# One stream step on one core: the sample moved from chunk 3 to chunk 2, fewer kept weights, the second norm's splits put ahead, v transposed one tile later

## The chip, the cores and the metric

One core of a Trainium2 chip runs the whole kernel. The metric is the device time of one execution in microseconds, the median of several.

## What is computed

One layer of a streaming encoder on 2048 prompt tokens (no history) and a sample of 8 sequences of 16 tokens, each with its own states and caches. The width is 1024, the feed-forward width 2816, all in float32:

```python
u = rms_norm(x, norm_mix) @ w_in                 # one projection, columns split among 4 mixers
z, xbc, dt_raw, q, k, v, u_sc, u_cc = jnp.split(u, IN_SPLITS, axis=-1)
ya, ssm_buf_new, h_new = mixer_ssd(z, xbc, dt_raw, ssm_buf, h0, ...)   # conv of 4 taps, then a scan in blocks
yb = swa_prompt(q, k, v, swa_sinks)              # or swa_sample(q, k, v, k_cache, v_cache, swa_sinks)
yc, sc_new = mixer_shortconv(u_sc, sc_buf, sconv_w)                    # conv of 3 taps
yd, cc_new = mixer_conformer(u_cc, cc_buf, ...)                        # conv of 31 taps
x = x + jnp.concatenate([ya, yb, yc, yd], axis=-1) @ w_out
hf = rms_norm(x, norm_ffn)
x = x + (jax.nn.silu(hf @ w_gate) * (hf @ w_up)) @ w_down
```

The results are the final norm of both token groups and the new states, among them the last 3 columns of `xbc` (`o_xc_s` for the sample) and the last 30 of the conformer's input (`o_g_s`).

## The kernel before

The 16 blocks of 128 prompt tokens are cut into five chunks, c0 to c4, and the sample's 128 tokens are appended to one of them. Tokens lie along the free axis, features along the partitions. Every matrix product is made from operands split into a high and a low part, in three matmuls for each 128 rows: high by high, high by low, low by high (`group`, L239 to L241). A split is a copy on ACT and a subtraction on DVE (`split`, L199; `split_w` for weights, L204, both with the subtraction through `tt`, L184). A weight tile of 128 x 1024 is loaded by SP into one of two buffers `fr` and split into one of three buffers `w`; or it was written in its split form to DRAM by POOL the first time (`kept<-w`, L227, 1 MB) and is later loaded from there (`w<-kept`, L219), without a split. `keep` says which tiles of w_in are stored so: in chunk 1 those with an even number, in chunk 2 those with an odd one.

The stages in order: proj_in of c0 and part of c1; for c0 and c1 in turn, proj_out, proj_in of the next chunk with the second norm beside it, and the chunk's FFN with the mixers of the next chunk woven in; proj_out of c2; the FFN of c2 merged with proj_in of c3, whose mixers run in it; the same for c4; then an FFN for the tokens of c3 and c4 together, with seven products in place of eight. proj_in runs over the 21 tiles of w_in, in c1 and c2 in the order of `W_IN_TILES` (c0, h0, b0, c1, h1, b1, k, v, B, C, dt, q0, q1, x0, x1, z0, z1, g0, a0, g1, a1; even and odd numbers in turn), in c3 and c4 in the order `SPREAD` (g0, a0, B, C, x0, x1, ...).

The tiles h, B, C, x0, x1 and a go through a buffer `raw` (two of them): DVE copies the last columns of the chunk before into its head (`raw_tiles`, L394), POOL loads the sample's history (L397, from `sst`, `xst` or `gst`), ACT or DVE puts in the new columns (`evac_raw`, L420 and L422), DVE keeps the last columns (`keep_raw`, L427), POOL stores the sample's last columns (L436, `o_xc_s<-raw`, 12 KB in pieces of 12 bytes), and the taps of the convolution are multiplied in one by one (`conv`, L187 and L192), for the prompt and the sample apart. A `raw` buffer is free for the next tile when its store has landed. For a0 and a1 DVE also doubles the loaded history (L191).

The second norm (`norm2`) makes the eight operands of the FFN: a multiply on DVE into `nt` and a split into `act`, two of them after each of four units of proj_in. v is transposed on TensorE right after its tile is computed (L569), from a copy that ACT makes into `ut` (L560).

A scheduler sets each engine's order when the kernel is built: it follows the order in the code, and `tc.high_priority(offset=n)` puts what is under it ahead as though it had been written n instructions earlier (AHEAD is 1000, used for weight loads with their splits, SOON is 120). Each engine and each DMA queue (SP's and POOL's) then runs in its order, and an instruction that waits holds all behind it.

The largest chunk has 512 tokens, `TM`; the FFN of the last two chunks works on halves of N = 448 tokens, whose operands come back from DRAM in tiles `ht`.

Of the kernel before, what the change touches and what calls it, by code (L numbers as in the profile page):

```python
# [17 lines left out]
P = 128  # L18
# [47 lines left out]


class Cfg:
    def __init__(self, chunks=(2, 4, 4, 3, 3), sample_in=3, nff=22, rounds=(4, 4, 4, 4, 3, 3),
                 rounds_last=(4, 4, 4, 4, 1, 3, 2), nfirst=3):  # L70
        self.chunks = chunks
        self.sample_in = sample_in
        self.nff = nff
        self.rounds = rounds
        self.rounds_last = rounds_last

        self.nfirst = nfirst
        self.np_tiles = sum(chunks)
        self.tokens = self.np_tiles * P + NS
        self.tmax = max(c * P + (NS if i == sample_in else 0) for i, c in enumerate(chunks))  # L80
# [38 lines left out]
def stream_step(ctx: ExitStack, tc: tile.TileContext, cfg, x, xr, w_in, w_out, w_gu, w_down, tab, con, dist_p, dist_s,  # L119
# [86 lines left out]
        return d  # L206

    kept = {}  # L210

    def load_w(src, shape, key=None, store=False):
# [15 lines left out]
        return pat(d[:, 0, :n]), pat(d[:, 1, :n])  # L228

    def keep(c, n):  # L230
        return c["i"] in (1, 2) and (c["i"] == 2 or n % 2 == 0)

    tail = [None]

# [212 lines left out]
    def after_in(c, name, ps):  # L447
# [18 lines left out]
        elif name[0] == "c":  # L466
            t = mk(up, [P, TM], "ut", bufs=B["ut"])[:, :T]
            act.activation(t, ps[:, :T], AF.Copy)
            u[name] = t
        elif name[0] == "h":  # L470
            j = int(name[1])
            rp, rs = raw_tiles(c, 2, hist["s"][j], sst[j])
            t = u["c" + name[1]]
            tt(rp[:, 2:2 + Tp], t[:, :Tp], ps[:, :Tp], ALU.mult)
            if Ts:
                tt(rs[:, :, 2:], sv(t[:, Tp:]), sv(ps[:, Tp:T]), ALU.mult)
            keep_raw(c, rp, rs, 2, hist["s"][j], o_s_p[j], o_s_s[j])
            m = mk(up, [P, TM], "mix", bufs=B["mix"])
            conv(c, m, rp, rs, [T_("sw", 3 * j + k) for k in range(3)], None)
            u["y" + name[1]] = m  # L480
        elif name[0] == "b":
            m = u["y" + name[1]]
            tt(m[:, :T], m[:, :T], ps[:, :T], ALU.mult)
        elif name in ("x0", "x1", "B", "C"):
            j = ("x0", "x1", "B", "C").index(name)
            rp, rs = raw_tiles(c, 3, hist["xs"][j], xst[j])
            evac_raw(c, ps, rp, rs, 3)
            keep_raw(c, rp, rs, 3, hist["xs"][j], o_xc_p[j], o_xc_s[j])
            m = mk(up, [P, TM], "x" + name)
            conv(c, m, rp, rs, [H_("xw", 4 * j + k) for k in range(4)], H_("xb", j))  # L490
            t = mk(up, [P, TM], "ut", bufs=B["ut"])[:, :T]
            act.activation(t, m[:, :T], AF.Tanh)
            stt(m[:, :T], t, 1.0, m[:, :T], ALU.add, ALU.mult)
            u[name] = m
        elif name == "dt":
            xx = mk(up, [P, TM], "ut", bufs=B["ut"])[:, :T]
            e = mk(up, [P, TM], "ut", bufs=B["ut"])[:, :T]
            l = mk(up, [P, TM], "acum")[:, :T]
            p = mk(up, [P, TM], "pk")[:, :T]

            act.activation(xx, ps[:, :T], AF.Identity, bias=T_("dtb"))
            act.activation(e, xx, AF.Abs)
            act.activation(e, e, AF.Exp, scale=-1.0)
            act.activation(l, e, AF.Ln, bias=1.0)
            ts(p, e, 0.2, ALU.mult)
            for cst in (-0.25, 1.0 / 3.0, -0.5, 1.0):
                stt(p, p, cst, e, ALU.add, ALU.mult)
            tt(p, p, l, ALU.subtract)
            stt(p, e, 0.05, p, ALU.is_lt, ALU.mult)
            tt(l, l, p, ALU.add)  # L510
            stt(xx, xx, 0.0, l, ALU.max, ALU.add)

            ts(e, xx, A, ALU.mult)
            for b in range(c["nt"]):
                bs_ = slice(b * P, (b + 1) * P)
                dve.tensor_tensor_scan(out=l[:, bs_], data0=ones, data1=e[:, bs_], initial=0.0, op0=ALU.mult,
                                       op1=ALU.add)
            if Ts:
                dve.tensor_tensor_scan(out=l[:, Tp:], data0=C_("rsts", P), data1=e[:, Tp:], initial=0.0,
                                       op0=ALU.mult, op1=ALU.add)  # L520
            u["acum"] = l

            for b in range(c["nt"]):
                act.activation(p[:, b * P:(b + 1) * P], l[:, b * P:(b + 1) * P], AF.Exp, scale=-1.0,
                               bias=l[:, b * P + P - 1:b * P + P])
            if Ts:
                lv, pv = sv(l[:, Tp:]), sv(p[:, Tp:])
                tt(pv, bc(lv[:, :, DEC_T - 1:], [P, DEC_B, DEC_T]), lv, ALU.subtract)
                act.activation(p[:, Tp:], p[:, Tp:], AF.Exp)
            tt(p, p, xx, ALU.mult)  # L530

            ts(p, p, C_("pick", 3)[:, 2:3], ALU.mult)
            stt(p, xx, C_("pick", 3)[:, 1:2], p, ALU.mult, ALU.add)
            stt(p, l, C_("pick", 3)[:, 0:1], p, ALU.mult, ALU.add)
            u["pk"] = p
        elif name in ("q0", "q1"):
            t = mk(up, [P, TM], name)
            act.activation(t[:, :Tp], ps[:, :Tp], AF.Copy, scale=0.125)
            if Ts:

                if name == "q0":
                    u["qs"] = mk(up, [P, DEC_B, 2, DEC_T], "qs")
                act.activation(u["qs"][:, :, int(name[1])], sv(ps[:, Tp:T]), AF.Copy, scale=0.125)
            u[name] = t
        elif name == "k":
            t = mk(up, [P, P + TM], "k")
            if prev["k"]:
                pool.tensor_copy(t[:, :P], hk)
            act.activation(t[:, P:P + T], ps[:, :T], AF.Copy)
            if c["i"] != last:  # L550
                pool.tensor_copy(hk, t[:, Tp:Tp + P])
            prev["k"] = True
            if Ts:
                pool.dma_start(o_k_s, t[:, P + Tp:P + T])
            if c["i"] == last:
                pool.dma_start(o_k_p, t[:, Tp:Tp + P])
            u["k"] = t
        elif name == "v":
            t = mk(up, [P, TM], "ut", bufs=B["ut"])[:, :T]
            act.activation(t, ps[:, :T], AF.Copy)  # L560
            if Ts:
                pool.dma_start(o_v_s, t[:, Tp:])
            if c["i"] == last:
                pool.dma_start(o_v_p, t[:, Tp - P:Tp])

            pv = mk(px, [P, 512], "px")
            nt = T // P
            for b in range(nt):
                pe.transpose(pv[:, b * P:(b + 1) * P], t[:, b * P:(b + 1) * P], ident)  # L569
            vt = mk(up, [P, 5, P], "vt", bufs=1)  # L570
            if prev["v"]:
                dve.tensor_copy(vt[:, 0], hv)
            act.activation(vt[:, 1:1 + nt].rearrange("p a b -> p (a b)"), pv[:, :T], AF.Copy)
            if c["i"] != last:
                dve.tensor_copy(hv, vt[:, c["nt"]])
            prev["v"] = True
            u["vt"] = vt
        elif name in ("z0", "z1"):
            t = mk(up, [P, TM], name)
            act.activation(t[:, :T], ps[:, :T], AF.Tanh, scale=0.5)  # L580
            stt(t[:, :T], t[:, :T], 1.0, ps[:, :T], ALU.add, ALU.mult)
            u[name] = t
# [290 lines left out]
    def proj_in(c, names):  # L873
        c.setdefault("u", {})

        def unit(name):
            wh, wl = load_w(w_in[W_IN_TILES.index(name)], [KT, P], W_IN_TILES.index(name), keep(c, W_IN_TILES.index(name)))
            ps = mk(pm, [P, 512], "pm")
            group(ps, c["T"], [(wh[:, k], wl[:, k], c["xn"][k]) for k in range(KT)])
            after_in(c, name, ps)  # L880

        return [lambda n=n: unit(n) for n in names]
# [27 lines left out]
    def norm2(c):  # L910
        T = c["T"]
        r = rstd_of(c["ss"], T, D)
        yield
        r = spread(r, T)
        c["hf"] = []
        for k in range(KT):
            t = mk(np_, [P, TM], "nt", bufs=B["nt"])[:, :T]
            stt(t, c["x2"][k][:, :T], T_("gffn", k), r, ALU.mult, ALU.mult)
            d = mk(ap, [P, 2, TM], "act", F32R)
            split(d, t, T)  # L920
            c["hf"].append(d)
            if k in (1, 3, 5):
                yield
        yield
# [333 lines left out]
    def operand(j, h):  # L1258
        if j >= cfg.nff - 2:
            d = hs[j, h]  # L1260
        else:
            with tc.high_priority(offset=AHEAD):
                d = mk(ht, [P, 2, N], "ht", F32R)
                sync.dma_start(d.bitcast(F32), hmem[j][:, h])
        return d[:, 0], d[:, 1]

# [192 lines left out]
```

## Time and profile before

| | |
|---|---|
| time, three runs | 2401.3, 2409.1 and 2415.3 us; median 2409.1 |
| the profiled execution | 2405.4 us, span 2403.7 |
| granted clock of TensorE, mean | 0.990 |
| proj_in of c2 | 508 to 626 us |
| FFN of c1 with the mixers of c2 | 626 to 1018 |
| proj_out of c2 | 1018 to 1057 |
| proj_in of c3 merged with the FFN of c2 | 1057 to 1431 |
| proj_out and proj_in of c4 | 1431 to 1680 |

Times in a view count from the span's start. PE is TensorE's matmuls, PEld its weight loads, DVE, ACT, POOL and SP the other engines and SP's queue. A row of a wait names the instruction that waited, after the arrow the engine and instruction that released it, then the total, the number of times and the longest.

### The profile page before, as it was taken

How to read it: one execution, taken by the hardware profiler on the slowest of the kernel's cores; microseconds unless marked ns; L12 is line 12 of the kernel's file. 1: busy time of each engine (PE TensorE's matmuls, PEld its weight loads, DVE VectorE, ACT ScalarE, POOL GpSimd, SP SyncE). 2: the span in 40 equal slices, each digit the busy share in tenths (PEclk: the TensorE clock that was granted, in tenths of full speed). 3: DMA queues.
4: the chain of work that ended last, by engine and by line, in shares of the span. 5: the costliest groups of instructions: out<-in, count | busy, mean ns of one | idle time of the engine just before them, and what ended most of it. 6: DMA issues, size and time to landing. Idle time of an engine off the chain costs nothing.

```text
span 2403.7 us, 32336 instructions
## 1 busy us (share of the span) xinstructions
PE 2348.2 (98%) x12370; PEld 2039.3 (85%) x12370; DVE 1580.0 (66%) x2980; ACT 883.2 (37%) x1500; POOL 148.0 (6%) x266
## 2 busy tenths in 40 slices
PE   8999999999999999997999999999999999999997
PEld 7888999888888888886778788988879999999997
DVE  7997998865884456657573554775777666763424
ACT  6544545533333333323212232232344444442221
POOL 1000000000000000001010000000001000000000
PEclk9999999999999999998999999999999999999998
DMA  6547454567555555555444436643633333239663
GB/s 224 198 162 246 149 159 156 167 244 280 188 185 168 183 176 171 198 215 162 150 151 145 149 123 227 226 162 130 206 106 118 131 115 124 94 129 327 198 184 119
DMA packets 132667, 417.37 MB, mean 174 GB/s; under 512 B 12848, under 2 KB 48592, under 8 KB 115360
## 3 DMA queue, kind: packets, MB, share of 16 engines
q1 hardware_dynamic: 114736, 324.57, 41.4%
q0 software_dynamic: 17776, 90.73, 9.9%
q8 instruction: 97, 1.59, 0.3%
q14 instruction: 58, 0.48, 0.1%
HBM read 324.07 MB, written 91.18 MB: 173 GB/s over the span
## 4 chain that ended last, share of the span: by engine, by line
PE 49%; DVE 3%; DMA 2%; ACT 0%; issue 0%; POOL 0%; DVEq 0%; SPq 0%; ACTq 0%; POOLq 0%
PE pm L239 8%; PE pm L240 7%; PE pm L241 7%; PE pm L1167 7%; PE pm L1169 7%; PE pm L1168 7%; PE px L1167 1%; PE px L1169 1%; PE px L1168 1%; DMA o_xc_s<-raw 1%; DVE mix L187 1%; DMA nt<-xr 0%; DVE x L187 0%; DMA act<-kc 0%; DMA w<-kept 0%
## 5 line engine op out<-in xcount | busy, mean ns | idle before, releaser
L239 PE MATMUL pm<-act,w 128*128 128x512 f32 (+2 forms) x2216 | 799.9, 361 | 7.0 <-DMA w<-kept 3.2
L240 PE MATMUL pm<-act,w 128*128 128x512 f32 (+2 forms) x2216 | 791.9, 358 | 10.3 <-DVE act L184 10.3
L241 PE MATMUL pm<-act,w 128*128 128x512 f32 (+2 forms) x2216 | 790.3, 357 | 1.2 <-DVE w L184 1.2
L204 ACT ACTIVATE w<-fr 128x1024 fp32r<-128x1024 f32 (+2 forms) x380 | 393.5, 1036 | 885.4 <-PE pm L241 522.6
L184 DVE TENSOR_TENSOR w<-fr,w 128x1024 fp32r<-128x1024 f32 (+2 forms) x380 | 454.3, 1196 | 281.3 <-ACT w L204 279.6
L239 PEld LDWEIGHTS pm<-act,w 128*128 128x128 f32 x2216 | 418.5, 189 | 71.4 <-issue 5.0
L240 PEld LDWEIGHTS pm<-act,w 128*128 128x128 f32 x2216 | 419.2, 189 | 65.8 <-DVE act L184 11.2
L241 PEld LDWEIGHTS pm<-act,w 128*128 128x128 f32 x2216 | 418.8, 189 | 56.9 <-DVE w L184 1.6
L1167 PE MATMUL pm<-hf,w 128*128 128x448 f32 x616 | 225.3, 366 | 0.1
L1168 PE MATMUL pm<-hf,w 128*128 128x448 f32 x616 | 225.2, 366 | 0.0
L1169 PE MATMUL pm<-hf,w 128*128 128x448 f32 x616 | 225.0, 365 | 0.0
L187 DVE SCALAR_TENSOR_TENSOR mix<-raw,tabh,mix 128x384 f32<-128x384 f32 (+3 forms) x360 | 202.7, 592 | 2.1
L239 PE MATMUL pm<-h,w 128*128 128x512 f32 (+1 forms) x528 | 191.7, 364 | 7.0 <-ACT hf L199 3.3
L240 PE MATMUL pm<-h,w 128*128 128x512 f32 (+1 forms) x528 | 188.6, 358 | 0.0
L241 PE MATMUL pm<-h,w 128*128 128x512 f32 (+1 forms) x528 | 188.5, 358 | 0.0
L184 DVE TENSOR_TENSOR x<-x,pm 128x512 f32<-128x512 f32 (+2 forms) x184 | 108.3, 599 | 71.2 <-PE pm L241 63.3
L187 DVE SCALAR_TENSOR_TENSOR ft<-ft,pm 128x512 f32<-128x512 f32 (+1 forms) x132 | 78.5, 595 | 107.4 <-PE pm L241 86.2
L1167 PEld LDWEIGHTS pm<-hf,w 128*128 128x128 f32 x616 | 115.7, 188 | 10.2 <-ACT g L1181 0.9
L1169 PEld LDWEIGHTS pm<-hf,w 128*128 128x128 f32 x616 | 115.7, 188 | 9.3
L1168 PEld LDWEIGHTS pm<-hf,w 128*128 128x128 f32 x616 | 115.7, 188 | 9.2
L239 PEld LDWEIGHTS pm<-h,w 128*128 128x128 f32 x528 | 101.0, 192 | 25.0 <-ACT hf L199 3.7
L240 PEld LDWEIGHTS pm<-h,w 128*128 128x128 f32 x528 | 101.2, 192 | 14.5 <-issue 0.7
(292 smaller groups left out, 2562.8 us busy)
## 6 DMA issues: line engine op xcount, KB each, us to landing
w<-kept SPq DMA_DIRECT2D x83, 1024.0 KB, 5.2
fr<-w_gu SPq DMA_DIRECT2D x154, 512.0 KB, 3.3
kept<-w POOLq DMA_DIRECT2D x51, 1024.0 KB, 6.3
fr<-w_down SPq DMA_DIRECT2D x84, 512.0 KB, 3.8
fr<-w_in SPq DMA_DIRECT2D x52, 512.0 KB, 4.0
fr<-w_out SPq DMA_DIRECT2D x40, 512.0 KB, 3.4
hm<-h POOLq DMA_DIRECT2D x44, 448.0 KB, 4.4
ht<-hm SPq DMA_DIRECT2D x40, 448.0 KB, 5.1
```

Source lines behind the costliest of these rows:

```text
L184: return eng.tensor_tensor(out=out, in0=a, in1=b, op=op)
L187: return eng.scalar_tensor_tensor(out=out, in0=a, scalar=s, in1=b, op0=op0, op1=op1)
L204: act.activation(d[:, 0, :n], raw, AF.Copy)
L239: pe.matmul(ps[:, :T], wh, o[:, 0, :T], start=(i == 0), stop=False)
L240: pe.matmul(ps[:, :T], wh, o[:, 1, :T], start=False, stop=False)
L241: mm = pe.matmul(ps[:, :T], wl, o[:, 0, :T], start=False, stop=(i == n - 1))
L1167: pe.matmul(ps[:, :N], wh[:, i], a, start=first and i == 0, stop=False, skip_group_check=True)
L1168: pe.matmul(ps[:, :N], wh[:, i], b, start=False, stop=False, skip_group_check=True)
L1169: mm = pe.matmul(ps[:, :N], wl[:, i], a, start=False, stop=(i == n - 1), skip_group_check=True)
```

## The change

Five things are changed.
- The chunks have 2, 4, 3, 4 and 3 blocks of prompt tokens in place of 2, 4, 4, 3 and 3, and the sample is appended to c2 in place of c3. The lengths with the sample stay 256, 512, 512, 512 and 384.
- Only the even w_in tiles of c1 are stored in split form. Ten stores fewer are made in c2, and c3 and c4 load and split ten more tiles each.
- v is transposed after the matmuls of the next tile.
- The second norm's multiplies and splits are under `high_priority(offset=SOON)`.
- An `ht` tile has room for 512 tokens, of which 448 are used.

```diff
-    def __init__(self, chunks=(2, 4, 4, 3, 3), sample_in=3, nff=22, rounds=(4, 4, 4, 4, 3, 3),
+    def __init__(self, chunks=(2, 4, 3, 4, 3), sample_in=2, nff=22, rounds=(4, 4, 4, 4, 3, 3),
...
     def keep(c, n):
-        return c["i"] in (1, 2) and (c["i"] == 2 or n % 2 == 0)
+        return c["i"] == 1 and n % 2 == 0
...
-            pv = mk(px, [P, 512], "px")
-            nt = T // P
-            for b in range(nt):
-                pe.transpose(pv[:, b * P:(b + 1) * P], t[:, b * P:(b + 1) * P], ident)
...
+            def turned():
+
+                pv = mk(px, [P, 512], "px")
+                nt = T // P
+                for b in range(nt):
+                    pe.transpose(pv[:, b * P:(b + 1) * P], t[:, b * P:(b + 1) * P], ident)
...
+            c["turn"] = turned
...
             group(ps, c["T"], [(wh[:, k], wl[:, k], c["xn"][k]) for k in range(KT)])
+
+            if "turn" in c:
+                c.pop("turn")()
             after_in(c, name, ps)
...
         for k in range(KT):
-            t = mk(np_, [P, TM], "nt", bufs=B["nt"])[:, :T]
-            stt(t, c["x2"][k][:, :T], T_("gffn", k), r, ALU.mult, ALU.mult)
-            d = mk(ap, [P, 2, TM], "act", F32R)
-            split(d, t, T)
+            with tc.high_priority(offset=SOON):
+                t = mk(np_, [P, TM], "nt", bufs=B["nt"])[:, :T]
+                stt(t, c["x2"][k][:, :T], T_("gffn", k), r, ALU.mult, ALU.mult)
+                d = mk(ap, [P, 2, TM], "act", F32R)
+                split(d, t, T)
...
             with tc.high_priority(offset=AHEAD):
-                d = mk(ht, [P, 2, N], "ht", F32R)
+                d = mk(ht, [P, 2, TM], "ht", F32R)[:, :, :N]
```

In the changed kernel lines behind `split_w` have moved by one to six (L394 is now L393, L436 L435, L752 L754).

How the orders differ, at three places. A name has its buffer number behind it; DMASW and DMAHW in the brackets are waits for DMAs of POOL's and SP's queue.

First, DVE at the start of c3's proj_in, where the operands of c2's FFN are made. `raw_1559` belongs to C, `raw_1568` to x0, `nt` and `act` to the second norm, `w_1584` to weights. Before:

```order
L187 SCALAR_TENSOR_TENSOR xC_1560_10091<-raw_1559_10084,tabh_5_92,xC_1560_10091 128x128 [waits DVE_49]
L184 TENSOR_TENSOR w_1584_10247<-fr_1583_10245,w_1584_10247 128x1024 [waits DMAHW3_49,DMAHW6_49,DMAHW1_49,Activation_49]
L187 SCALAR_TENSOR_TENSOR xC_1560_10091<-ut_1561_10100,xC_1560_10091 128x512 [waits Activation_49]
L184 TENSOR_TENSOR act_1563_10105<-nt_1562_10103,act_1563_10105 128x512
L187 SCALAR_TENSOR_TENSOR nt_1564_10108<-x2_1516_9773,tab_1_84,px_1543_9970 128x512
L394 COPY raw_1568_10140<-hx0_7_97 128x3 [waits DMASW7_49]
L192 TENSOR_SCALAR xx0_1569_10147<-raw_1568_10140,tabh_5_92 128x128 [waits DMASW0_49,Activation_49]
...
L184 TENSOR_TENSOR act_1565_10110<-nt_1564_10108,act_1565_10110 128x512 [waits Activation_49]
```

and now:

```order
L187 SCALAR_TENSOR_TENSOR nt_1558_10206<-x2_1507_9841,tab_1_84,px_1555_10196 128x512
L184 TENSOR_TENSOR act_1557_10203<-nt_1556_10201,act_1557_10203 128x512 [waits Activation_49]
L187 SCALAR_TENSOR_TENSOR nt_1565_10250<-x2_1513_9886,tab_1_84,px_1555_10196 128x512
L184 TENSOR_TENSOR act_1559_10208<-nt_1558_10206,act_1559_10208 128x512 [waits Activation_49]
L187 SCALAR_TENSOR_TENSOR nt_1567_10255<-x2_1518_9922,tab_1_84,px_1555_10196 128x512 [waits DVE_49]
L184 TENSOR_TENSOR act_1566_10252<-nt_1565_10250,act_1566_10252 128x512 [waits Activation_49]
L187 SCALAR_TENSOR_TENSOR nt_1575_10310<-x2_1523_9962,tab_1_84,px_1555_10196 128x512 [waits DVE_49]
L184 TENSOR_TENSOR act_1568_10257<-nt_1567_10255,act_1568_10257 128x512 [waits Activation_49]
L187 SCALAR_TENSOR_TENSOR nt_1577_10315<-x2_1528_10002,tab_1_84,px_1555_10196 128x512 [waits DVE_49]
L184 TENSOR_TENSOR act_1576_10312<-nt_1575_10310,act_1576_10312 128x512 [waits Activation_49]
```

The multiplies and splits, between which stood the copy into x0's `raw` and x0's convolution, now follow each other.

Second, DVE in c2's proj_in, from B's convolution (`xB`) to the weight split of x0's tile. `raw_981` and `raw_986` (before) and `raw_975` and `raw_980` (now) are those of x0 and x1. Before:

```order
L427 COPY hx2_9_99<-raw_953_6127 128x3 [waits Activation_49]
L192 TENSOR_SCALAR xB_954_6131<-raw_953_6127,tabh_5_92 128x512
L187 SCALAR_TENSOR_TENSOR xB_954_6131<-raw_953_6127,tabh_5_92,xB_954_6131 128x512 [waits DVE_49] x3
L394 COPY raw_981_6335<-hx0_7_97 128x3 [waits DVE_49]
L187 SCALAR_TENSOR_TENSOR xB_954_6131<-ut_955_6136,xB_954_6131 128x512 [waits Activation_49]
...
L192 TENSOR_SCALAR xC_961_6175<-raw_960_6171,tabh_5_92 128x512
L187 SCALAR_TENSOR_TENSOR xC_961_6175<-raw_960_6171,tabh_5_92,xC_961_6175 128x512 [waits DVE_49] x3
L394 COPY raw_986_6374<-hx1_8_98 128x3 [waits DVE_49]
L187 SCALAR_TENSOR_TENSOR xC_961_6175<-ut_962_6180,xC_961_6175 128x512 [waits Activation_49]
L184 TENSOR_TENSOR w_978_6305<-fr_977_6303,w_978_6305 128x1024 [waits DMAHW1_49,DMAHW7_49,DMASW1_49,Activation_49]
```

and now, C's taps, in pieces of 384 and 128 tokens, left out:

```order
L187 SCALAR_TENSOR_TENSOR xB_950_6140<-raw_949_6133,tabh_5_92,xB_950_6140 128x384 [waits DVE_49]
L187 SCALAR_TENSOR_TENSOR xB_950_6140<-raw_949_6133,tabh_5_92,xB_950_6140 128x128 [waits DVE_49]
L393 COPY raw_975_6353<-hx0_7_97 128x3 [waits DMASW7_49,DVE_49]
L187 SCALAR_TENSOR_TENSOR xB_950_6140<-ut_951_6149,xB_950_6140 128x512 [waits Activation_49]
L426 COPY hx3_10_100<-raw_955_6182 128x3 [waits Activation_49]
L192 TENSOR_SCALAR xC_956_6189<-raw_955_6182,tabh_5_92 128x384
...
L187 SCALAR_TENSOR_TENSOR xC_956_6189<-raw_955_6182,tabh_5_92,xC_956_6189 128x128 [waits DVE_49]
L393 COPY raw_980_6399<-hx1_8_98 128x3 [waits DMASW1_49,DVE_49]
L187 SCALAR_TENSOR_TENSOR xC_956_6189<-ut_957_6198,xC_956_6189 128x512 [waits Activation_49]
L184 TENSOR_TENSOR w_973_6325<-fr_972_6323,w_973_6325 128x1024 [waits DMAHW1_49,DMAHW0_49,Activation_49]
```

The copies into the heads of the `raw` buffers (L394, now L393) now wait for a DMA of POOL's queue too, and x0's weight split stands behind the second of them. On POOL, the same stretch has stores of split weights before:

```order
L227 DMA kept958_6144<-w_957_6141 128x2048 [waits DMASW2_49,DVE_49]
L227 DMA kept971_6245<-w_970_6242 128x2048 [waits DMASW3_49,DVE_49]
L227 DMA kept979_6308<-w_978_6305 128x2048 [waits DMASW4_49,DVE_49]
L227 DMA kept991_6391<-w_990_6388 128x2048 [waits DMASW5_49,DVE_49]
L227 DMA kept999_6456<-w_998_6453 128x2048 [waits DMASW6_49,DVE_49]
```

and now the loads and stores of the sample, those of B, C, x0, a0, x1 and a1:

```order
L435 DMA o_xc_s<-raw_949_6133 1024x1x3 [waits DMASW7_49,Activation_49]
L396 DMA raw_975_6353<-xst 128x8x3 [waits DMASW2_49,DMASW7_49,DMASW0_49,DVE_49]
L435 DMA o_xc_s<-raw_955_6182 1024x1x3 [waits Activation_49]
L396 DMA raw_980_6399<-xst 128x8x3 [waits DMASW4_49,DMASW1_49,DVE_49]
L435 DMA o_xc_s<-raw_975_6353 1024x1x3 [waits Activation_49]
L396 DMA raw_996_6540<-gst 128x8x30 [waits DMASW3_49,DMASW0_49,DVE_49]
L435 DMA o_xc_s<-raw_980_6399 1024x1x3 [waits DMASW5_49,Activation_49]
L396 DMA raw_1005_6610<-gst 128x8x30 [waits DMASW5_49,DMASW6_49,DMASW2_49,DVE_49]
```

Each load into a `raw` stands between two stores, and waits for the one that holds that buffer.

Third, TensorE at v in c2's proj_in: `pm_947` (before) is v's own product, `pm_952` that of B, and now `pm_946` is B's and `pm_954` C's. Before:

```order
L240 MATMUL pm_947_6064<-act_844_5406,w_945_6059 128x512
L241 MATMUL pm_947_6064<-act_844_5406,w_945_6059 128x512
L239 MATMUL pm_952_6102<-act_808_5232,w_951_6100 128x512 [waits DMAHW2_49]
L240 MATMUL pm_952_6102<-act_808_5232,w_951_6100 128x512
L241 MATMUL pm_952_6102<-act_808_5232,w_951_6100 128x512
L239 MATMUL pm_952_6102<-act_810_5238,w_951_6100 128x512
L569 MATMUL px_949_6091<-con_2_85,ut_948_6089 128x128 [waits Activation_49]
...
L240 MATMUL pm_952_6102<-act_810_5238,w_951_6100 128x512
L241 MATMUL pm_952_6102<-act_810_5238,w_951_6100 128x512
```

and now:

```order
L238 MATMUL pm_946_6099<-act_844_5406,w_945_6097 128x512
L239 MATMUL pm_946_6099<-act_844_5406,w_945_6097 128x512
L240 MATMUL pm_946_6099<-act_844_5406,w_945_6097 128x512
L569 MATMUL px_947_6124<-con_2_85,ut_944_6094 128x128 [waits Activation_49]
...
L238 MATMUL pm_954_6157<-act_808_5232,w_953_6154 128x512 [waits DVE_49]
L239 MATMUL pm_954_6157<-act_808_5232,w_953_6154 128x512
L240 MATMUL pm_954_6157<-act_808_5232,w_953_6154 128x512 [waits DVE_49]
```

The transposes stood four matmuls into B's tile, and now stand behind all of it.

More of the change, by code (lines that the diff above doesn't have):

```diff
@@ L564, in after_in @@
                 pool.dma_start(o_v_p, t[:, Tp - P:Tp])
-            pv = mk(px, [P, 512], "px")
-            nt = T // P
-            for b in range(nt):
[L569 to L577, printed above, removed]
+            def turned():
[3 more added lines that the diff above has]
+                    pe.transpose(pv[:, b * P:(b + 1) * P], t[:, b * P:(b + 1) * P], ident)
+                vt = mk(up, [P, 5, P], "vt", bufs=1)
+                if prev["v"]:
+                    dve.tensor_copy(vt[:, 0], hv)
+                act.activation(vt[:, 1:1 + nt].rearrange("p a b -> p (a b)"), pv[:, :T], AF.Copy)
+                if c["i"] != last:
+                    dve.tensor_copy(hv, vt[:, c["nt"]])
+                prev["v"] = True
+                u["vt"] = vt
+            c["turn"] = turned
         elif name in ("z0", "z1"):
```

## The prediction

> **What bounds the kernel now.** I read the page's shares first, then what TensorE waits for, then the places of those waits in the timeline and the chain.
>
> ```profile
> span 2403.7 us, 32336 instructions
> PE 2348.2 (98%) x12370; PEld 2039.3 (85%) x12370; DVE 1580.0 (66%) x2980; ACT 883.2 (37%) x1500; POOL 148.0 (6%) x266
> ```
>
> TensorE is busy for 98% of the span, and the change leaves its matrix work as it is (the same five chunk lengths in tokens, 256, 512, 512, 512, 384, in the same places; they are numbered 0 to 4 below). So it can gain only from the 55 us in which TensorE stands still and from stretches at half clock. The waits of TensorE (total, times, longest):
>
> ```profile
> PE pm L240 <- DVE act L184: 10.3, 2, 6.2
> PE pm L239 <- DMA w<-kept: 3.2, 1, 3.2
> PE pm L239 <- ACT act L199: 2.9, 1, 2.9
> PE px L569 <- ACT ut L560: 2.9, 3, 1.3
> PE px L752 <- DMA act<-kc: 2.7, 1, 2.7
> ...
> PE pm L241 <- DVE w L184: 1.2, 2, 0.8
> ```
>
> The timeline of TensorE gives their places; the bracket is the idle time ahead of a row.
>
> ```profile
> 1089.82 0.39 PE L239 MATMUL pm<-act,w 128*128 128x512 f32 x1
> ...
> 1093.22 0.39 PE L239 MATMUL pm<-act,w 128*128 128x512 f32 x1
> 1097.67 0.79 PE L240 MATMUL pm<-act,w 128*128 128x512 f32 x1 [4.06 <-DVE act L184]
> ...
> 1106.01 0.80 PE L240 MATMUL pm<-act,w 128*128 128x512 f32 x1 [6.23 <-DVE act L184]
> ...
> 1110.56 0.80 PE L239 MATMUL pm<-act,w 128*128 128x512 f32 x1 [2.90 <-ACT act L199]
> ...
> 1340.14 0.42 PE L752 MATMUL px<-act,qs 64*32 64x128 f32 x8 [2.68 <-DMA act<-kc]
> ```
>
> From 1089.82 to 1093.22 there are 15 starts, 0.227 us each; a tile of 24 matmuls at 512 tokens takes 5.44 us. Then 4.06 + 6.23 + 2.90 = 13.2 us are lost at the first gate of chunk 2's FFN, which runs among chunk 3's proj_in and whose operands (`act`, the second norm's splits) aren't there. Busy time by stretch (start:end, length, PE, PEld, DVE, ACT, POOL, granted clock, DMA share, GB/s):
>
> ```profile
> 508.00:626.00 118.00, 117.14 (x525) 96.85 (x524) 70.44 (x131) 41.24 (x68) 6.12 (x11) 1.00 0.70 259
> 626.00:1018.00 392.00, 392.00 (x1831) 319.42 (x1831) 251.93 (x427) 135.31 (x221) 26.40 (x52) 1.00 0.54 180
> 1116.00:1431.00 315.00, 310.99 (x1556) 251.78 (x1555) 181.69 (x435) 85.69 (x173) 17.61 (x33) 0.99 0.43 152
> 1476.00:1680.00 204.00, 203.69 (x1105) 180.36 (x1104) 140.19 (x313) 62.35 (x132) 11.66 (x24) 1.00 0.54 183
> 1095.60:1116.10 20.50, 9.20 (x19) 6.00 (x20) 12.39 (x28) 5.53 (x12) 3.54 (x4) 0.50 0.47 123
> 1341.40:1348.20 6.80, 6.80 (x34) 4.87 (x35) 4.47 (x15) 1.31 (x6) 0.29 (x1) 0.50 0.05 19
> 1715.20:1722.00 6.80, 6.76 (x33) 5.70 (x34) 4.48 (x13) 2.24 (x5) 0.00 (x0) 1.00 0.22 74
> ```
>
> The fifth stretch ran at a clock of 0.50, so about half of its 9.20 busy us was lost too: 4.6. The sixth follows the `kc` wait and lost 3.4 of 6.80; the last, behind the wait for the kept tile, lost nothing. Why the operands came late at 1097, the chain there tells (start, length, what):
>
> ```profile
> 1075.33 9.70 DMA o_xc_s<-raw
> ...
> 1085.12 0.17 DVE raw L394
> ...
> 1089.23 6.81 DMA o_xc_s<-raw
> ...
> 1096.67 0.88 POOL raw L397
> 1097.55 11.84 DMA o_xc_s<-raw
> ```
>
> The sample's stores of 12 KB (`o_xc_s`) hold one of the two `raw` buffers for 7 to 12 us. DVE's small copy into the next `raw` (L394) waits for that in DVE's order, and the norm's splits stand behind it.
>
> **The change part by part.**
>
> *Chunk 3 loses the sample.* No `o_xc_s` stands there any more, and the order has all eight splits of the second norm in one piece on DVE, ahead of any convolution of chunk 3. Both removers act on one stall, so it is counted once: −13.2 − 4.6 = −17.8. What is late next:
>
> ```profile
> L187 DVE SCALAR_TENSOR_TENSOR nt<-x,tab,px 128x512 f32<-128x512 f32 x8 | 5.9, 743 | 0.0
> ...
> L184 DVE TENSOR_TENSOR act<-nt,act 128x512 fp32r<-128x512 f32 x8 | 5.5, 689 | 0.3 <-ACT act L199 0.3
> ```
>
> These sixteen are 11.4 us of DVE, and TensorE has five tiles of chunk 3's proj_in ahead of the gate (27 us at 5.44), so nothing is. Ends: 0 (something else holds DVE) and −17.8.
>
> *Transposes of v one tile later.* The three waits at L569, 2.9 us, go: ACT's copy into `ut` then has a whole tile to finish, and the transposed v is read only by the attention of the next stage. −2.9; the end above is 0.
>
> *The sample's attention moves into the FFN of chunk 1* (626 to 1018 before). The `kc` load lands after:
>
> ```profile
> act<-kc POOLq DMA_DIRECT2D x1, 512.0 KB, 7.8
> ...
> 1332.32 0.53 POOL L741 DMA_DIRECT2D act<-kc  x1
> ```
>
> Before, it was asked for at 1332.3, 5.1 us ahead of its use (1340.14 less 2.68). Now its buffer comes free in the middle of a1's tile, the last of chunk 2's proj_in, and by the order that half, a gate tile and an up tile follow before the use: about 13 us. −2.7 for the wait and −3.4 for the half clock: −6.1, ends 0 and −6.1. The extra DVE work of the sample there fits: DVE is busy 252 of 392 us. In POOL's order the sample's loads stand between the stores of chunk 1's first gate and up tiles, each of which holds one of three `w` buffers; their own buffers come free while a1 still runs, before the next store has anything to send: 0, at worst one landing, +7.8.
>
> *Ten tiles of w_in no longer kept.* Ten stores of 1 MB go from chunk 2's proj_in (rows below); in chunks 3 and 4 ten kept loads each become a load of 512 KB and a split.
>
> ```profile
> L204 ACT ACTIVATE w<-fr 128x1024 fp32r<-128x1024 f32 x42 | 44.5, 1059 | 138.0 <-PE pm L241 121.4 <-issue 13.3 <-DMA fr<-w_out 3.3
> L184 DVE TENSOR_TENSOR w<-fr,w 128x1024 fp32r<-128x1024 f32 x42 | 51.6, 1228 | 30.9 <-ACT w L204 30.7
> ...
> kept<-w POOLq DMA_DIRECT2D x10, 1024.0 KB, 6.4
> w<-kept SPq DMA_DIRECT2D x9, 1024.0 KB, 7.2
> fr<-w_in SPq DMA_DIRECT2D x7, 512.0 KB, 4.1
> ```
>
> That is 20 × 1.23 = 24.6 us of DVE and 20 × 1.06 = 21.2 of ACT, 12.3 and 10.6 per chunk. DVE has 133 us free of 315 in the one stage and 64 of 204 in the other, and the splits are ordered ahead of their use: 0, the cover being that spare time. Without it, up to +24.6. The one wait for `w<-kept` (3.2) is in the last such stage; half of the w_in tiles before it now come by the shorter load, and I take −1 (ends −3.2 and 0).
>
> *The sample in chunk 2's proj_in: the new cost.* Here no early order helps: B, C, dt, q0, q1, x0, x1, z0, z1, g0, a0, with two `raw` buffers. The landing times are those seen in chunk 3:
>
> ```profile
> L436 POOL DMA_DIRECT2D o_xc_s<-raw x4: 861/868/892, 1075.3 to 1111.0; - x4
> ...
> DMA to landing us min/median/max: 6.8/8.7/11.8
> ...
> L397 POOL DMA_DIRECT2D raw<-gst x2: 899/904/910, 671.3 to 1119.4; - x2
> ...
> DMA to landing us min/median/max: 3.1/5.2/7.4
> ...
> 1096.32 0.69 DVE L187 SCALAR_TENSOR_TENSOR xC<-ut,xC 128x512 f32<-128x512 f32 x1
> ```
>
> The three in the chain average 9.45, the median of four is 8.7; I take 9.0. With t = 0 at the store of B, TensorE, 1.5 us into C then, comes to x0 at 4 × 5.44 − 1.5 = 20.3.
> - 9.0: B's store has landed. DVE's copy into x0's `raw`, which waited for it, runs, and POOL issues x0's history load (0.9) and, behind it in POOL's order, C's store at 9.95.
> - 19.0: C's store has landed; DVE's copy into x1's `raw` runs. Behind it: one multiply of 0.69 and x0's weight split, 1.23, done at 20.9. TensorE wanted it at 20.3: **0.6**.
> - x1's kept tile is asked for behind the load that waits for the buffer this split frees: issue 21.3, landing 6.9 later at 28.2 (kept loads have 7.2 in that stage). TensorE is through with x0 at 25.9: **2.3**.
> - x0's store goes at 31.7, lands at 40.7; the load of the conformer's history behind it (5.2, the middle of its two landings of 3.1 and 7.4) at 45.9; DVE's doubling of it and g0's split (1.23) make 48 with the hand-overs, TensorE being there at 45: **3.0**.
> - The same chain with x1's store costs **1.1** each at a0 (kept load) and g1 (split), and **0.8** at a1.
>
> Sum +8.8, in single gaps of at most 3.0. DVE stands waiting some 23 us meanwhile and has 118 − 70 = 48 to spare, so the rest catches up. Each us more of landing adds some 4.4 (two stores ahead of x0, one more store and load each ahead of g0 and g1, less what waits anyway); at 6.8, the shortest of the four, the stall is nearly 0, and at 11.8, the longest, 21. The small stores of chunk 3 were slow at a DMA share of 0.47; here it was 0.70 with the kept stores in, so I see no reason for short ones. For the clock, the gap of 2.68 at 1340 cost 3.4, and that of 3.2 at the kept tile nothing: one of two. I take +2.5 for the two larger gaps here, between 0 and 5.
>
> The Trainium skill ("TensorE: Matmul & The Clock Gate", "HAM oscillation — how this bites in real kernels") says that the clock falls when an idle gap exceeds about 3.4 us. The trace has a fall after 2.68 us, so it goes further than the rule here; by the rule the term would be 0 and not 2.5.
>
> *The `ht` tiles sliced from a larger one* load the same bytes at the same place in the order; they share addresses with other old tiles, which moves no wait: 0, ends ±1.
>
> Sum: −17.8 − 2.9 − 6.1 − 1 + 8.8 + 2.5 = −16.5. The profiled execution took 2405.4 us (span 2403.7), 3.7 under the median of 2409.1 and within the runs (2401.3 to 2415.3). −16.5 gives 2389 from the one and 2393 from the other: **2391**.
>
> **The rivals.** About 0.5%, 12 us, is what a measurement of this kernel tells from no change.
> - *No stall in chunk 2.* If the stores land in 6.8 us or less, that chain hides and −28 stands: about 2379. For it: with ten kept stores gone, the POOL queue and the DMA engines are freer. Against: they weren't crowded in chunk 3 either. The Trainium skill ("DMA: Bandwidth & Descriptors", "Anatomy of one DMA — SWDGE (gpsimd) path") fits a gpsimd DMA by 2.0 us plus bytes over 436 KB per us, an estimate of 2.03 us for 12,288 bytes, by which this rival would be the forecast. The trace disagrees by a factor of three to six.
> - *The stall only moves.* The four stores and the two history loads stall chunk 2 as long as they did chunk 3, with the clock halved: −28 + 13 + 5 = −10, or with the 21 of the longest landing and 7 of clock 0: 2397 to 2409. It needs landings of 10 to 12 us, well inside the measured spread.
> - *Slower.* Landings near 14 us in chunk 2's proj_in, because its loads of 1 MB hold the engines (DMA share 0.70 against 0.47 in the stretch measured): 8.8 + 5 × 4.4 = 31 of stall, and some 10 at half clock: +14, about 2421. Equal time comes at some 11.8, and slower by 12 us at about 13.5; none of the four landed that late.
> - *The twenty splits show.* Should they lie on TensorE's path, +24.6 makes 2414 to 2417. For it: splits wait in DVE's order behind convolutions; against: before, 42 such splits in these stages left TensorE only 1.2 us of waiting (L241's weights).
>
> **How the numbers follow.** The forecast (−12 to −22) has 0.45; no stall 0.15; the stall only moves 0.28; slower by landings 0.05; the splits in part or in full 0.07, half of it slower by 12 us and half within the bound. Faster by over 0.5% is then 0.60, but the own-run gap of 3.7 puts a little of the forecast at the bound: 0.58; within 0.5% 0.33, slower 0.09. The range from the rival without a stall to that where it only moves, 2376 to 2411, leaves out about 2 in 10.
>
> **What would show it.** Right: no row of TensorE waiting on `act` L184 or L199 at the first gate of chunk 2's FFN, and full clock there; no wait at L569 and at `kc`; in chunk 2's proj_in (508 to 635) gaps of 0.5 to 3 us ahead of x0, x1, g0, a0 and g1, released by DVE's weight split or a kept load, DVE waiting on `o_xc_s`, and that stage some 9 to 11 us longer. Wrong: landings of `o_xc_s` under 7 or over 11 us, a clock of 0.5 there, or new waits for `w` L184 after 1100.

## The result, and the profile after

The changed kernel takes 2396.9 us (median of ten runs, 2393.5 to 2399.0), the kernel before 2409.8 (ten runs, 2401.3 to 2417.5). The ratio is 0.9946, with a 95% interval of 0.9931 to 0.9960: 13 us faster, 10 to 17. The profiled execution took 2397.2 us, 8.3 less than that of before, which lay 4.4 under its kernel's median of ten.

The page, and what TensorE waits for (total, times, longest):

```profile
span 2395.4 us, 32332 instructions
PE 2345.5 (98%) x12370; PEld 2038.7 (85%) x12370; DVE 1601.0 (67%) x3000; ACT 901.7 (38%) x1520; POOL 146.7 (6%) x256
```

```profile
PE pm L238 <- DMA w<-kept: 14.4, 5, 5.1
...
PE pm L240 <- DVE w L184: 2.9, 3, 1.7
```

No row is left for `act` (13.2 before), for v's `ut` (2.9) and for `kc` (2.7). In their place stand 14.4 us on kept tiles (3.2 before). Where, the timeline of TensorE tells:

```profile
557.06 0.77 PE L238 MATMUL pm<-act,w 128*128 128x512 f32 x1 [5.14 <-DMA w<-kept]
...
593.81 0.47 PE L238 MATMUL pm<-act,w 128*128 128x512 f32 x1 [0.66 <-DMA w<-kept]
...
609.63 0.77 PE L238 MATMUL pm<-act,w 128*128 128x512 f32 x1 [4.67 <-DMA w<-kept]
...
1526.10 0.44 PE L240 MATMUL pm<-act,w 128*128 128x384 f32 x1 [1.70 <-DVE w L184]
...
1540.96 0.44 PE L238 MATMUL pm<-act,w 128*128 128x384 f32 x1 [0.75 <-DMA w<-kept]
...
1706.59 0.77 PE L238 MATMUL pm<-act,w 128*128 128x512 f32 x1 [3.13 <-DMA w<-kept]
```

Three are in chunk 2's proj_in, 10.5 us: the tiles of B, x1 and z1. Stretches around them, and around the first gate of chunk 2's FFN (columns as in the prediction):

```profile
555.90:562.70 6.80, 5.64 (x13) 4.46 (x14) 3.03 (x12) 1.99 (x5) 1.83 (x3) 0.50 0.70 239
607.10:613.90 6.80, 4.27 (x10) 3.44 (x11) 3.98 (x11) 0.00 (x0) 1.76 (x2) 0.50 0.19 30
1706.20:1709.60 3.40, 3.01 (x7) 2.46 (x8) 2.55 (x8) 1.15 (x2) 0.00 (x0) 0.50 0.49 165
1089.00:1112.00 23.00, 23.00 (x105) 19.01 (x104) 20.58 (x35) 11.23 (x21) 0.00 (x0) 1.00 0.54 187
```

At the gate TensorE is busy throughout, at full clock. Half clock follows both long waits of chunk 2 and costs half of 5.64 and of 4.27, 5.0 in all, and 1.5 more at 1706.

The sum on the profiled executions: gone are 17.8 at the gate, 2.9 at v and 6.1 at `kc`, 26.8. New are 10.5 + 5.0 in chunk 2, 2.5 in chunk 4 (1526 and 1541) and 1.5 of clock at 1706: 19.5. That makes −7.3 of the −8.3.

Why the kept tiles are late: DMAs issued in chunk 2's proj_in of the changed kernel (KB each, median us to landing):

```profile
w<-kept SPq DMA_DIRECT2D x9, 1024.0 KB, 9.6
...
raw<-xst POOLq DMA_DIRECT2D x4, 12.0 KB, 5.7
...
o_xc_s<-raw POOLq DMA_DIRECT2D x4, 12.0 KB, 8.1
o_s_s<-raw POOLq DMA_DIRECT2D x2, 8.0 KB, 8.0
```

and two pieces of the chain there, the two kept loads on which TensorE waited at 593 and 609:

```profile
588.10 5.58 DMA w<-kept
...
599.30 10.19 DMA w<-kept
```

The same 1 MB took 5.6 us, and 10.2 when x0's store `o_xc_s`, issued 0.5 us ahead of it, was under way. Of the others in this stage those with no small store beside them took 4.8, 5.0 and 5.5 us, one beside v's store of 64 KB 7.6, and those issued while a store in pieces of 8 or 12 bytes was under way 9.6 to 10.3. B's own load, 10.7, is a case apart: it was issued at 546.25, just as h1's store `o_s_s` (537.2, 9.1 us) landed. What that store held up were the loads ahead of it in SP's queue, of 512 KB (issued at 542.5) and 256 KB (543.0), which took 10.1 and 10.2 us. While they were out the DMA engines moved 12 GB/s (the last column), and 322 in the same stretch of the kernel with packed stores (described below), where a kept load was out:

```profile
543.00:546.00 3.00, 3.00 (x15) 2.49 (x14) 0.16 (x1) 0.72 (x2) 0.00 (x0) 1.00 0.42 12
```

```profile
543.00:546.00 3.00, 3.00 (x15) 2.49 (x14) 0.76 (x2) 0.96 (x3) 0.00 (x0) 1.00 1.01 322
```

That became the theory to test: a store in 1024 pieces of 8 or 12 bytes holds up the big loads beside it.

### The profile page after: what moved, and what is told of

It reads as the page before. It is cut to its first block, busy times and chain, and to the rows that moved or that the text cites. A ratio compares the mean times of both kernels' runs of the same rounds, so it can differ in the third digit from the quotient of the medians.

```text
span 2395.4 us, 32332 instructions
## 1 busy us (share of the span) xinstructions
PE 2345.5 (98%) x12370; PEld 2038.7 (85%) x12370; DVE 1601.0 (67%) x3000; ACT 901.7 (38%) x1520; POOL 146.7 (6%) x256
## 4 chain that ended last, share of the span: by engine, by line
PE 63%; issue 8%; DVE 2%; DMA 2%; ACT 0%; POOL 0%; DVEq 0%; POOLq 0%; ACTq 0%; SPq 0%
PE pm L238 12%; PE pm L239 12%; PE pm L240 12%; PE pm L1173 7%; PE pm L1175 7%; PE pm L1174 7%; PE px L1173 2%; PE px L1175 1%; PE px L1174 1%; DMA w<-kept 1%; DVE mix L187 0%; PE px L703 0%; DVE x L187 0%; PE px L721 0%; PE px L731 0%
## 5 line engine op out<-in xcount | busy, mean ns | idle before, releaser
L238 PE MATMUL pm<-act,w 128*128 128x512 f32 (+2 forms) x2216 | 801.2, 362 | 16.1 <-DMA w<-kept 14.4
L204 ACT ACTIVATE w<-fr 128x1024 fp32r<-128x1024 f32 (+3 forms) x400 | 414.7, 1037 | 933.7 <-PE pm L240 551.0
L184 DVE TENSOR_TENSOR w<-fr,w 128x1024 fp32r<-128x1024 f32 (+3 forms) x400 | 478.2, 1196 | 276.9 <-ACT w L204 274.8
L184 DVE TENSOR_TENSOR x<-x,pm 128x512 f32<-128x512 f32 (+2 forms) x184 | 108.0, 597 | 76.5 <-PE pm L240 69.5
```

What stands on the lines that cost most here:

```text
L184: return eng.tensor_tensor(out=out, in0=a, in1=b, op=op)
L204: act.activation(d[:, 0, :n], raw, AF.Copy)
L238: pe.matmul(ps[:, :T], wh, o[:, 0, :T], start=(i == 0), stop=False)
```

## The experiments

All ratios are to the kernel before, run on the same chip in between (medians there 2414.9 to 2417.5).

**The move and the stores of split weights.** The move alone:

```diff
-    def __init__(self, chunks=(2, 4, 4, 3, 3), sample_in=3, ...
+    def __init__(self, chunks=(2, 4, 3, 4, 3), sample_in=2, ...
```

> The kernel before with only the sample moved from chunk 3 to chunk 2; the ten stores of 1 MB in chunk 2, the early transposes and the old order of the norm stay. Theory: the stalls of chunk 3 (17.8) and at kc (6.1) go; in chunk 2 the sample's 12-byte pieces slow the kept loads of 1 MB beside them, and the ten stores of 1 MB on top of that: 12 to 25 us of stall there, two to four stretches at half clock: ratio 0.997 to 1.003, slower than the whole change. Rival: the stores of 1 MB do nothing, the stall in chunk 2 is the 10.5 us of the changed kernel: ratio 0.994 to 0.996, transposes included.

Measured: 1.0001 (0.9990 to 1.0013), as the theory had it. The move alone brings nothing. In chunk 2's proj_in TensorE stands still for 21.6 us by the timeline, twice as long as in the changed kernel; its waits over the whole span:

```profile
PE pm L239 <- DMA w<-kept: 19.5, 6, 4.1
...
PE pm L241 <- DVE w L184: 7.2, 4, 4.2
```

The changed kernel with the ten stores put back:

```diff
-        return c["i"] == 1 and n % 2 == 0
+        return c["i"] in (1, 2) and (c["i"] == 2 or n % 2 == 0)
```

> The changed kernel with the ten odd w_in tiles of chunk 2 stored again, so that chunks 3 and 4 load them in split form. Theory: the stores of 1 MB on POOL's queue beside the sample's small ones make the stall of chunk 2 longer than 10.5 us, 15 to 25, and the small waits near 1526 and 1541 (2.5 us, a weight split) go: 3 to 12 us slower than the changed kernel (ratio 0.996 to 1.0). Rival: the stores have no part in chunk 2's stall; only the 2.5 us in chunk 4 go: ratio 0.9930 to 0.9945.

Measured: 1.0017 (1.0006 to 1.0028), 17 us more than the changed kernel, beyond what I expected. Its waits, and the DMAs of the stage:

```profile
PE pm L238 <- DMA w<-kept: 26.5, 8, 9.2
PE pm L240 <- DVE w L184: 8.4, 4, 5.7
```

```profile
kept<-w POOLq DMA_DIRECT2D x10, 1024.0 KB, 10.4
w<-kept SPq DMA_DIRECT2D x9, 1024.0 KB, 8.7
o_xc_s<-raw POOLq DMA_DIRECT2D x4, 12.0 KB, 9.3
o_s_s<-raw POOLq DMA_DIRECT2D x2, 8.0 KB, 12.2
```

So leaving out the ten stores is what makes the move pay. And from the other side, the kernel before with only these stores left out (the same line, in the kernel before):

> The kernel before with only the ten stores of odd w_in tiles in chunk 2 left out, so that chunks 3 and 4 load and split them. Theory: with no sample in chunk 2 these stores disturbed nothing there (0.9 us of waits in that stage), and the twenty splits and smaller loads hide but for some 2 us: between 2 us faster and 5 us slower than before (ratio 0.999 to 1.002). Rival: the stores cost some 17 us in any case: ratio about 0.993.

Measured: 0.9970 (0.9956 to 0.9984), 7 us faster, between the two. Its kept loads in chunk 2 land in 4.8 us (7.2 before), but there was no stall there that this could remove. Where the 7 us come from is left open.

**The order of the second norm.** The changed kernel without the priority (`with tc.high_priority(offset=SOON)` taken out of `norm2`):

> The changed kernel with the second norm's multiplies and splits back in their old order (no priority). Theory: with the sample out of chunk 3 nothing there holds DVE for long, so the priority adds nothing: no wait of TensorE on act at the first gate of chunk 2's FFN over 1 us, and the time of the changed kernel, 2396.9 +- 3 us (ratio to before 0.993 to 0.996). Rival: the splits wait behind convolutions on DVE without any sample, and the stall of 13.2 us with 4.6 at half clock comes back in part: 5 to 18 us more than the changed kernel (ratio 0.997 to 1.002).

Measured: 0.9895 (0.9880 to 0.9910), faster than the changed kernel, which neither theory had. No wait on `act` comes back, so for chunk 3 the priority isn't needed once the sample is gone. But the function also serves chunk 1's FFN, whose norm stands beside chunk 2's proj_in: without the priority B's kept load is issued at 542.1 in place of 546.3, and the 5.1 us wait at B is missing, though the load is as slow (11.0 us). The two traces show what delays the issue. With the priority, the norm's splits stand ahead on DVE, h0's sample columns reach `raw` at 528.5 in place of 520.7, and the store `o_s_s` goes at 528.8 in place of 521.0. The kept load issued at 530.2 then runs beside it and takes 10.3 us; without the priority that store has landed, and the load takes 4.7. The loads behind it in SP's order, B's among them, are late from there on. So by these traces this cost of the priority, too, comes from a small store; the run with packed stores and the old order, below, bears it out.

The kernel before with the priority alone:

> The kernel before with only the priority on the second norm's multiplies and splits; the sample stays in chunk 3. Theory: the stall of 13.2 us is the splits' place behind DVE's copies into raw, not the stores as such, so it goes here too, with its 4.6 at half clock: 14 to 18 us faster than before (ratio 0.9925 to 0.994), and faster than the whole change. Rival: the stores then hold the next weight splits or kept loads of chunk 3 instead, and 6 to 13 us of stall remain at other rows: 0 to 8 us faster (ratio 0.9965 to 1.0).

Measured: 0.9991 (0.9980 to 1.0001): no gain. The theory fell, the rival held, and the rows of TensorE say how:

```profile
1106.85 0.77 PE L239 MATMUL pm<-act,w 128*128 128x512 f32 x1 [7.90 <-DMA w<-kept]
...
1123.59 0.47 PE L239 MATMUL pm<-act,w 128*128 128x512 f32 x1 [3.62 <-DMA w<-kept]
```

The waits on `act` are gone, and 11.5 us of waits on kept tiles stand in their place: these two loads took 15.0 and 12.4 us, beside the same small stores. DVE's order was only the first of two ways in which these stores stop TensorE.

**The pieces.** First the changed kernel again, beside those that differ from it by a copy:

> The changed kernel once more, beside the three kernels that differ from it by a copy: both theories expect the ratio already measured, 0.993 to 0.996, and a stall of 9 to 12 us in chunk 2's proj_in on kept loads.

Measured: 0.9940 (0.9925 to 0.9955), with 5.8, 1.0, 4.6 and 1.0 us of waits on kept tiles in chunk 2. Then a copy with the pieces left small, which is to take away only the hold of `raw`:

```diff
             if scale is None:
-                pool.dma_start(out_s, rs[:, :, DEC_T:])
+                t = mk(up, [P, DEC_B, 4], "kr")
+                pool.tensor_copy(t[:, :, :H], rs[:, :, DEC_T:])
+                pool.dma_start(out_s, t[:, :, :H])
```

> The changed kernel, in which POOL first copies the sample's last columns from raw into a small tile of their own and the stores o_xc_s and o_s_s go from there, still in 1024 pieces of 8 or 12 bytes. The hold of raw by the store is gone, the small pieces stay. Theory (the pieces slow the kept loads of 1 MB that share the DMA engines with them, from about 5.3 us to about 10): DVE no longer waits on o_xc_s, but kept loads still land in 9 to 11 us and 7 to 12 us of stall remain: within 4 us of the changed kernel. Rival, that of the prediction (DVE held by raw makes weight splits and kept loads late): the stall falls to 3 us or less: 8 to 14 us faster than the changed kernel.

Measured: 0.9919 (0.9902 to 0.9937); 5 us under the changed kernel by the medians' ratios, with intervals that overlap. That lies between the theory (4 at most) and the rival (8 at least), nearer the theory. DVE no longer waits on `o_xc_s`; the copy has one buffer, and POOL waited once, 5.7 us, for it to come free. Two waits on kept tiles are left in chunk 2, 3.35 and 4.85 (in an execution 5 us under this kernel's median), and the stores land as late as ever:

```profile
L437 POOL DMA_DIRECT2D o_xc_s<-kr x4: 855/860/923, 565.5 to 602.4; - x4
...
DMA to landing us min/median/max: 7.7/8.5/11.2
```

The load on which TensorE waited 4.85 took 11.4 us. The one of the 3.35 landed in 6.3, but was issued late, behind a load of 256 KB that took 14.5 beside a small store.

The same with a contiguous copy:

```diff
-                pool.dma_start(out_s, rs[:, :, DEC_T:])
+                t = mk(up, [P, DEC_B * 3], "kr")[:, :DEC_B * H]
+                pool.tensor_copy(sv(t), rs[:, :, DEC_T:])
+                pool.dma_start(out_s.rearrange("p b t -> p (b t)"), t)
```

> As the kernel with the copy, but the copy is contiguous, so that each store goes in 128 pieces of 64 or 96 bytes. Theory of the pieces: kept loads beside a store of o_xc_s land in 5 to 6.5 us and not in 10; the stall of 4.7 us at the last kept tile and its half clock go, that at B, beside the history loads in pieces of 12 bytes, stays at least in part: 5 to 9 us faster than the changed kernel. Rival of the hold: the same as with the copy in small pieces, within 2 us of it.

Measured: 0.9873 (0.9857 to 0.9889), 16 us under the changed kernel. The stores' landings, chunk 2's proj_in as a stretch, and its DMAs:

```profile
L437 POOL DMA_DIRECT2D o_xc_s<-kr x4: 538/550/552, 562.0 to 594.7; - x4
...
DMA to landing us min/median/max: 1.7/3.5/4.1
```

```profile
508.00:625.00 117.00, 117.00 (x525) 97.01 (x524) 77.83 (x181) 39.58 (x71) 15.71 (x27) 1.00 0.53 180
```

```profile
w<-kept SPq DMA_DIRECT2D x10, 1024.0 KB, 5.2
...
raw<-xst POOLq DMA_DIRECT2D x4, 12.0 KB, 4.9
...
o_xc_s<-kr POOLq DMA_DIRECT2D x4, 12.0 KB, 3.5
o_s_s<-kr POOLq DMA_DIRECT2D x2, 8.0 KB, 2.5
```

Nothing else differs from the copy with a stride: the same bytes, the same engine, the same place. In 128 pieces a store lands in 3.5 us and not 8.5, the kept loads in 5.2, and TensorE never stops in chunk 2, at full clock. The loads of the history still go in pieces of 12 bytes here, and TensorE waits for nothing beside them. Number and size of a store's pieces change together here; no run separates them (`o_xc_p`, 128 pieces of 12 bytes, landed in 2.8 to 6.8 us in the changed kernel), and why the small pieces do harm in the DMA engines no run shows. That they matter too I had half expected (the wait at B); packing them as well,

```diff
+                t = mk(up, [P, DEC_B * 3], "hin")[:, :DEC_B * H]
+                pool.dma_start(t, st_src.rearrange("p b t -> p (b t)"))
+                pool.tensor_copy(rs[:, :, :H], sv(t))
```

> In addition the history loads from xst and sst go in 128 pieces of 64 or 96 bytes into a small tile, from which POOL copies them into raw. Theory of the pieces: no kept load of chunk 2's proj_in takes over 7 us, the stall there falls from 10.5 to 2 us or less and the clock stays whole: 12 to 18 us faster than the changed kernel (ratio to before 0.986 to 0.990). Rival: loads in pieces of 12 bytes are too few to matter: within 2 us of the kernel with packed stores alone.

measured 0.9887 (0.9871 to 0.9904): no gain over the stores alone. (This kernel also has seven of the small buffers `n8` in place of nine.) Kept loads land in a median of 5.1.

Last, the packed stores in the kernel before, with nothing else changed:

> The kernel before with only the sample's stores o_xc_s and o_s_s sent from a small contiguous copy, in 128 pieces of 64 or 96 bytes; the sample stays in chunk 3. Theory of the pieces: the stall of 13.2 us at the first gate of chunk 2's FFN goes with its 4.6 at half clock, while the waits at v (2.9) and kc (2.7, and 3.4 at half clock) stay: 12 to 19 us faster than before (ratio 0.992 to 0.995), about what the whole change brings. Rival (the splits' place in DVE's order is what matters): 6 us or less faster.

Measured: 0.9916 (0.9896 to 0.9937), 20 us faster, a little over what was expected, and by its middle more than the whole change brings. The gate of chunk 2's FFN there, and the DMAs of chunk 3's start:

```profile
1090.00:1112.00 22.00, 21.21 (x94) 17.25 (x93) 18.28 (x42) 11.04 (x23) 3.27 (x6) 1.00 0.68 219
```

```profile
w<-kept SPq DMA_DIRECT2D x10, 1024.0 KB, 5.1
...
o_xc_s<-kr POOLq DMA_DIRECT2D x4, 12.0 KB, 3.7
```

13.2 us of waiting have become 0.8. The waits at v and `kc` stay in that kernel.

**What the change is worth without small pieces.** The ten stores put back, with packed stores of the sample:

> The changed kernel with both: the ten odd w_in tiles of chunk 2 stored again, and the sample's stores packed. With stores in small pieces the ten stores cost about 18 us. Theory: that was the meeting of both; with packed stores the stores of 1 MB hide in chunk 2's proj_in as they did before, stall there 3 us or less, and the small waits in chunk 4 go: within 4 us of the kernel with packed stores alone (ratio 0.9855 to 0.989). Rival: the stores of 1 MB cost the time by themselves: 8 to 18 us more than that kernel (ratio 0.9905 to 0.995).

Measured: 0.9877 (0.9856 to 0.9898), the same as without the ten stores. Their 17 us were the meeting of both. And the old order of the norm with packed stores:

> Packed stores, and the second norm in its old order. With small pieces the old order was some 9 us faster, since the stall at B's kept tile was missing. Theory: that stall came from the small pieces too, so with packed stores the order makes no difference: within 3 us of the kernel with packed stores alone (ratio 0.986 to 0.9885). Rival: the priority costs by itself, in the loads that it moves: 5 to 10 us faster still (ratio 0.983 to 0.985).

Measured: 0.9861 (0.9839 to 0.9882), 2384.3 us: not told apart from the kernel with packed stores alone, and with it the fastest of all that ran. The later transposes of v and the larger `ht` tile have no run of their own; of the first the missing waits at L569 are all that shows, and of the second nothing does.

## Why the prediction was right, and where its steps were not

The forecast was 2391 us in a range of 2376 to 2411, faster by over 0.5% at 0.58; 2396.9 came, and the interval of the ratio has the bound of 0.5% inside. By steps, on the profiled executions (−16.5 forecast, −8.3 measured):

- *Chunk 3 loses the sample, −17.8*: as forecast, TensorE without a pause at the gate. But "both removers act on one stall" was wrong for one of them: the norm's order removes nothing by itself, and isn't needed beside the move.
- *v, −2.9, and `kc`, −6.1*: both rows are gone, as forecast.
- *The ten tiles no longer kept, 0 and −1*: a step that failed, in both halves. The cover I named, DVE's spare time, held but for one split: ahead of 1526 DVE had waited 3.0 us for the store `o_xc_p` (128 pieces of 12 bytes) that held `raw`, and taps of two convolutions stood between that and the weights' split. With the 0.75 at 1541 that is +2.5. The wait at 1706 stayed, now with 1.5 at half clock. So +4 in place of −1. The other half is larger and stands in no term: kept, the ten stores would have cost 17 us beside the sample's. I listed them as removed and gave that no price.
- *The sample in chunk 2, +8.8*: 10.5. The size was near by luck, since the way was another. (The walk's own terms add to 8.9, and with its 0.6 TensorE is through with x0 at 26.3 and not 25.9, so that x1's 2.3 would be 1.9.) Of the six tiles that I named only x1 waited, 0.7 us and by the chain forecast, from the store over DVE's copy and a weight split to a late kept load; the 5.1 at B and the 4.7 at z1 I had nowhere. Stores landed in 7.8 to 8.5 us, under the 9.0 taken. DVE stood 15.4 us at its copies, as the row below has it, but the 4.7 us that I put on weight splits behind them (0.6, 3.0 and 1.1) are missing. What came were the kept loads, priced at 6.9 and taking 10. The walk took each DMA's time as its own; here a load's time depended on the store beside it.

```profile
DVE raw L393 <- DMA o_xc_s<-raw: 15.4, 4, 5.4
```

- *The clock, +2.5*: 5.0, since the waits came in two of about 5 us and not in six short ones.

Two of the signs of being wrong that I had named came: half clock in chunk 2's proj_in, and a wait for `w` L184 after 1100 (1.7 at 1526). So the total and the terms of what goes were right; the mechanism of the new costs was not.

By the Trainium skill ("TensorE: Matmul & The Clock Gate", "HAM oscillation — how this bites in real kernels"), whose bound is an idle gap of some 3.4 us, both gaps had to cost clock, and did. A gap of 2.0 us in the kernel without the priority also did, so the bound isn't a safe one here:

```profile
1521.72 0.50 PE L240 MATMUL pm<-act,w 128*128 128x384 f32 x1 [2.02 <-DVE w L184]
```

```profile
1522.00:1525.40 3.40, 3.40 (x12) 3.40 (x12) 3.40 (x7) 0.00 (x0) 0.00 (x0) 0.50 0.42 154
```

The rival without a stall in chunk 2 (about 2379) did not come true in this kernel; it did in the one with packed stores, 16 us lower. The fit of the Trainium skill that spoke for it ("DMA: Bandwidth & Descriptors", "Anatomy of one DMA — SWDGE (gpsimd) path", 2.03 us for these 12 KB as an estimate) is near the packed stores' 1.7 to 4.1 us; for the same bytes in pieces of 12 it is short by four times.

So the three terms of what goes held, and the misses of 5 (kept tiles), 1.7 (stall) and 2.5 (clock) all went one way: −16.5 + 9.2 = −7.3. Between the medians the change is −12.9, since the profiled execution of before, on which the sum was made, lay under its median and that of after on it; a forecast from −7.3 would have been 2400. That 2391 came within 6 us is thus in part luck: of the 9.2 that the sum missed, 4.6 were made up by where the two profiled executions lay.

## What to carry to other kernels

Look at the shape of a small store before its size: 12 KB in 1024 pieces delayed the large loads that were issued while it ran by about 5 us, and a copy into a contiguous tile of 96 bytes a partition, 0.2 to 0.4 us of POOL, took 20 us from the kernel before, where moving the work to another stage alone took nothing. When one change takes away a wait and the time stays, look at the next wait of the same cause, as the norm's order showed, where `act` became `w<-kept`. And a sum over durations from another stage has to ask what each DMA will run beside.

## What the runs showed of the hardware that was not expected

- A store to DRAM of 8 or 12 KB in 1024 pieces took 6.4 to 11.2 us from issue to landing in the kernel with the strided copy, and 1.7 to 4.1 in 128 pieces in the one with the contiguous copy. Loads of the same 1024 pieces did not slow the kept loads (5.2 with them, 5.1 without).
- Loads of 1 MB issued while such a store was under way took about 10 us and not 5, and stores of 1 MB, where they went beside such stores, a median of 10.4 and not the 6.4 of the kernel before. One load issued 1.5 us ahead of such a store (at 590.4 in the kernel with the strided copy) took 4.8. With both kinds of large transfer and packed stores the kept loads took 7.9, and TensorE waited only 1.8 us for them.
- Half clock followed waits of 2.0 and 3.1 us, and not waits of 1.7 (1526 in the changed kernel) and 3.2 (1715 in the kernel before).
